# Output projections of a decoder trunk: where their sums, rests, norm and loads stand in the queues

## The chip, the cores and the metric

One core of a Trainium2 chip runs the whole program. The metric is the device time of one execution in microseconds; the median of several runs is compared. TensorE (PE) multiplies, VectorE (DVE), ScalarE (ACT) and GpSimd (POOL) do the elementwise work, and SyncE (SP) starts most transfers. Each engine works through its own queue in order.

## The reference

x is 1024 rows of 1024 float32. There are two layers; the first has sparse attention, the second dilated attention over shared keys and values. What the change touches is the end of the attention and what follows it:

```python
    o = ...                                   # attention, (B, S, D_MODEL)
    mix = o.reshape(B, S, D_MODEL).astype(h.dtype) @ w_out
...
        x = x + mix.astype(x.dtype)
        x = x + swiglu(rmsnorm(x, norm_ffn[layer]), ffn_w_up[layer], ffn_w_down[layer]).astype(x.dtype)
    return rmsnorm(x, final_norm)

def rmsnorm(x, g):
    x32 = x.astype(jnp.float32)
    y = x32 * lax.rsqrt(jnp.mean(x32 * x32, axis=-1, keepdims=True) + RMS_EPS)
    return (y * g.astype(jnp.float32)).astype(x.dtype)
```

## The kernel before

**The projection as seven products.** Each layer's output projection (`out_proj`, from L1232) multiplies the attention's output, 1024 by 1024, with w_out in seven products of half the size instead of eight. `out_steps` (L1184) lists them: B11, B21, T1, T2, B22, T3, T4. The steps T1 to T3 and B22 need sums of the quarters of the attention's output; these are made by VectorE (L1226 to L1229), each in the `sums` argument of its step. Sums of the weights are made long before and lie in DRAM (`wS`).

**A block.** Each step has four blocks i, one for each 128 columns of its left operand. A block is four banks of PSUM, one for each 128 rows, with three matmuls a bank, so twelve matmuls of 128x512 (`mm3`, L203 to L205). Three, since both operands are split (`Pairs`, L900): ScalarE writes a rounded copy, "ph" (L910), and then another engine writes what the rounding left, "pl", called the **rest** here (L911). L203 multiplies copy with copy and needs no rest; L204 and L205 need them. The rests of the left operands, and of the weights of B11, B21 and B22, are VectorE's; those of the weights of T1 to T4 are POOL's (`made(t, nc.gpsimd)`), 16 a layer.

**The order of the work.** `staged` (L917) calls the preparation of a step and then the matmuls of the step before. Within an engine the program is not run in the order written: the framework simulates it with its own costs and puts each instruction into its engine's queue where that simulation has it, so a sum that needs only the attention's output may stand in VectorE's queue far ahead of the blocks that it is for. `after(x)` (L192) makes what is issued under it stand behind x in that order. Steps of one `group` share the banks dx0 to dx3 (group 0: B11, T2, T3, T4) or dr0, dr1, ux, uy (group 1: B21, T1, B22). After a step's last block VectorE adds each bank to the residual xr (L1217), and that add frees the bank for the next step. Step T4 (`whole=True`) is run bank by bank.

**The loads.** `load` fetches four weights of a step into a ring of 16 buffers "ow"; `rows` fetches tiles of xr. Both go through SP's queue, in the order B11, four tiles of xr, B21, T1, the other four tiles, T2, B22, T3, T4, unless the simulation moves them.

**The norm and the feed-forward.** `Blocks.half` (L1006) normalises four tiles of 128 rows: for each tile one square with its row sum on ScalarE (L1023), one on VectorE (L1024), an add (L1026), a square root on ScalarE (L1027), a reciprocal (L1028), and a scaling of each half (L1029 VectorE, L1030 ScalarE). Then TensorE transposes the tiles (L1002), and copies and rests (L165, L166) make the operands B11 and B21 of the feed-forward. `half` is called six times: in both output projections for the first four tiles (prepared between T3 and T4), in both feed-forwards for the other four (`ffn`, L1265), and twice at the end of layer 0 for the projections of layer 1 (`begin_B`, `project_B`). The feed-forward's first product is L1098; L1282 scales its weights by the norm's gain on POOL while the output projection runs. `dense` (L1409) opens eight banks by name and calls `out_proj`, then `ffn`. In layer 1 the attention's last part, with merges on VectorE and POOL (L1749, L1750), overlaps the first blocks of the projection.

Of the kernel before, what the change touches and what calls it, by code (L numbers as in the profile page):

```python
# [115 lines left out]
def trunk(ctx, tc, I, out):  # L116
# [785 lines left out]
    class Pairs:  # L902
# [5 lines left out]
        def __call__(self, src, eng=None):  # L908
            h, l = [self.p.tile([128, 512], F32R, name=n_, bufs=self.n) for n_ in ("ph", "pl")]
            nc.scalar.activation(h, src, AF.Copy)  # L910
            (eng or nc.vector).tensor_sub(l, src, f32(h))  # L911
            return h, l
# [74 lines left out]
    class Blocks:  # L987
# [18 lines left out]
        def half(self, xr, hf, banks, xn, junk=None, sums=None):  # L1006
# [4 lines left out]
            junk = junk or xn  # L1011

            def prep():
# [5 lines left out]
                for j in range(4):  # L1019
                    xt = xr[:, 4 * hf + j, :]  # L1020
                    ss = cst.tile([128, 2], F32, name="nss2", bufs=8)
                    rs = ss[:, 0:1]
                    nc.scalar.activation(junk[0][j], xt[:, lo], AF.Square, accum_out=rs)  # L1023
                    nc.vector.tensor_tensor_reduce(out=junk[1][j], in0=xt[:, hi], in1=xt[:, hi], scale=1.0, scalar=0.0,  # L1024
                                                   op0=OP.mult, op1=OP.add, accum_out=ss[:, 1:2])
                    nc.vector.tensor_add(rs, rs, ss[:, 1:2])  # L1026
                    nc.scalar.activation(rs, rs, AF.Sqrt, bias=eps, scale=1.0 / D)  # L1027
                    nc.vector.reciprocal(rs, rs)  # L1028
                    nc.vector.tensor_scalar(xn[0][j], xt[:, lo], rs, None, op0=OP.mult)  # L1029
                    nc.scalar.activation(xn[1][j], xt[:, hi], AF.Copy, scale=rs)  # L1030
                    if hf == 0:
                        self.rs.append(rs)
# [8 lines left out]
            return prep  # L1041
# [142 lines left out]
    def out_steps(spare, pairs, tmp, blocks, right, xr):  # L1184


        held = {}
        n = len(blocks)
        S_ = [tmp(i) for i in range(n)]

        def step(left, name, group, first, where, sums=None, whole=False):
            def operands(i):
                if sums is not None:
                    sums(i, *blocks[i])
                return pairs(left(i)), right(name, i)

            def prep():
                ready = [operands(0)]

                def run():  # L1200
# [8 lines left out]
                    for i, t in order:  # L1209
# [4 lines left out]
                        if i == n - 1:  # L1214
                            r, c = where
                            xs = xr[:, 4 * r + t, c * 512:(c + 1) * 512]
                            nc.vector.tensor_add(xs, xs, banks[t])  # L1217
# [14 lines left out]
    def out_proj(layer, pw, pp, p, xr, oT, w, x_src, norm):  # L1232
        pairs, made = Pairs(pp, 6), Pairs(p, 4)
        raw = {}

        def load(name):
            r, c = dict(B11=(0, 0), B21=(1, 0), B22=(1, 1), T1=(0, 0), T3=(0, 1), T4=(1, 0), T2=(1, 1))[name]
            cols = slice(c * 512, (c + 1) * 512)
            for i in range(4):
# [610 lines left out]
```

## Time and profile before

| what | value |
|---|---|
| median of 3 runs | 2850.45 us (2848.82 to 2853.51) |
| the profiled execution | 2848.69 us, of which the span is 2846.9 us |
| mean granted clock of TensorE | 0.987 |
| busy: PE, DVE | 2762.8 us (97%), 2234.1 us (78%) |
| busy: ACT, POOL | 1439.8 us (51%), 1467.4 us (52%) |
| layer 0: projection's first matmul, T4's first, feed-forward's first | 680.49, 757.76, 775.07 us |
| layer 1: the same | 2073.03, 2164.39, 2181.50 us |

Times in the views count from the start of the span. A row of the timeline has its start, its duration, engine, line and operation, and in brackets the idle time of the engine before it with what ended it. The granted clock is a share of the full clock. Where a row groups several instructions, their count stands behind an x.

### The profile page before, as it was taken

Reading aid. Unit: us, or ns where it says so; the run is one execution under the profiler, and the core shown is the slowest. Engines: PE = TensorE matmul, PEld = TensorE weight load, DVE = VectorE, ACT = ScalarE, POOL = GpSimd, SP = SyncE. Lnnn points to the kernel's source line nnn. Section 1 sums busy time; section 2 is a strip of 40 time slices with the busy share of each in tenths; the row PEclk is TensorE's granted clock in tenths of the full one; section 3 lists DMA queues with packets and bytes.
Section 4 is the critical chain, followed back from the end, with each engine's and each line's share of the span. In section 5 each row is a group of like instructions: output and inputs, shape, how many; then the busy total and the mean of one; then the engine's idle time right before and its main releaser. Section 6 shows DMA issues by size and latency. Waiting matters only on the chain.

```text
span 2846.9 us, 43111 instructions
## 1 busy us (share of the span) xinstructions
PE 2762.8 (97%) x14494; PEld 2234.4 (78%) x14494; DVE 2234.1 (78%) x4563; ACT 1439.8 (51%) x3174; POOL 1467.4 (52%) x1502
## 2 busy tenths in 40 slices
PE   9999999998999999999999999999989999999997
PEld 8988676776778888888778888777767788888886
DVE  5443888886878899989875877588888889888986
ACT  5431777774554343334464444577746434343434
POOL 3135655552665566556556787100035655655652
PEclk9999999999999999999999999999999999999998
DMA  8669443214022322231223555886440211111112
GB/s 245 203 205 294 113 127 104 73 49 168 25 71 67 85 64 67 62 81 58 77 81 106 172 158 156 261 240 183 125 150 26 71 60 54 54 56 60 52 45 78
DMA packets 292926, 315.15 MB, mean 111 GB/s; under 512 B 50428, under 2 KB 229677, under 8 KB 292704
## 3 DMA queue, kind: packets, MB, share of 16 engines
q1 hardware_dynamic: 272240, 249.40, 29.2%
q0 software_dynamic: 20464, 62.99, 7.2%
q8 instruction: 115, 1.88, 0.3%
q14 instruction: 107, 0.88, 0.1%
HBM read 243.96 MB, written 81.95 MB: 114 GB/s over the span
## 4 chain that ended last, share of the span: by engine, by line
PE 84%; DVE 7%; ACT 2%; issue 2%; POOL 1%; DMA 1%; SPq 1%; DVEq 0%; ACTq 0%; POOLq 0%
PE ux L1098 18%; PE uy L1098 14%; PE dx L950 7%; PE o L364 7%; PE pt L327 6%; PE dr L950 5%; PE dr L1098 4%; PE mm L203 3%; PE mm L204 3%; PE mm L205 3%; DVE pl L911 2%; PE s L746 2%; PE dx L1098 1%; PE s L834 1%; PE s L1678 1%
## 5 line engine op out<-in xcount | busy, mean ns | idle before, releaser
L911 DVE TENSOR_TENSOR pl<-oT,ph 128x512 fp32r<-128x512 f32 x337 | 352.2, 1062 | 73.9 <-PE dr L950 17.2
L910 ACT ACTIVATE ph<-oT 128x512 fp32r<-128x512 f32 x347 | 211.9, 627 | 206.7 <-PE ux L1098 53.4
L911 DVE TENSOR_TENSOR pl<-oTb,ph 128x512 fp32r<-128x512 f32 x233 | 213.0, 937 | 28.3 <-PE dr L950 17.3
L327 PE MATMUL pt<-ident,P 128*128 128x128 f32 x1536 | 229.5, 279 | 5.4 <-POOL P L730 2.5
L910 ACT ACTIVATE ph<-oTb 128x512 fp32r<-128x512 f32 x239 | 145.5, 627 | 169.5 <-PE ux L1098 53.0
L327 PEld LDWEIGHTS pt<-ident,P 128*128 128x128 f32 x1536 | 174.0, 141 | 64.8 <-issue 42.6
L730 POOL TENSOR_SCALAR P<-P,sm,gates 128x384 f32<-128x384 f32 (+7 forms) x256 | 183.1, 727 | 77.1 <-DVE sm L728 57.3
L955 DVE TENSOR_TENSOR xr<-xr,dr 128x512 f32<-128x512 f32 x320 | 204.0, 679 | 17.8 <-PE dr L950 17.6
L955 DVE TENSOR_TENSOR xr<-xr,dx 128x512 f32<-128x512 f32 x320 | 204.6, 678 | 2.6 <-PE dx L950 2.6
L1282 POOL TENSOR_TENSOR oT<-oT,gffn 128x512 f32<-128x512 f32 x92 | 112.7, 1234 | 146.6 <-DMA oT<-in_ffn_w_up_dram 104.7
L726 ACT ACTIVATE P<-P,m 128x384 f32<-128x384 f32 (+7 forms) x256 | 170.6, 668 | 34.4 <-DVE m L839 14.0
L330 DVE COPY pT<-pt 128x512 f32<-128x512 f32 (+1 forms) x224 | 143.3, 649 | 48.6 <-PE pt L327 45.9
L330 ACT COPY pT<-pt 128x512 f32<-128x512 f32 x192 | 110.0, 577 | 112.1 <-PE pt L327 111.7
L1282 POOL TENSOR_TENSOR oTb<-oTb,gffn 128x512 f32<-128x512 f32 x92 | 110.2, 1206 | 106.3 <-DMA oTb<-in_ffn_w_up_dram 81.5
L364 PE MATMUL o<-pT,V 128*64 128x256 f32 x1200 | 160.6, 391 | 2.4 <-ACT pT L330 1.8
L1660 ACT ACTIVATE P<-P,st 128x384 f32<-128x384 f32 (+2 forms) x256 | 139.4, 546 | 30.7 <-DVE st L1655 28.8
L1655 DVE CUSTOM_DVE_ANT_0 P<-s,T 128x384 f32<-128x384 f32 (+2 forms) x256 | 112.3, 478 | 9.8 <-PE pt L327 4.4
L364 PEld LDWEIGHTS o<-pT,V 128*64 128x64 f32 x1200 | 73.8, 136 | 52.2 <-issue 10.0
L950 PE MATMUL dx<-ph 128*128 128x512 f32 x320 | 107.5, 390 | 0.4 <-ACT ph L910 0.4
L835 DVE CUSTOM_DVE_ANT_0 P<-s,T 128x128 f32<-128x128 f32 (+3 forms) x192 | 99.7, 550 | 10.3 <-PE s L834 10.1
L950 PE MATMUL dx<-ph,pl 128*128 128x512 f32 x320 | 107.0, 389 | 0.0
L910 ACT ACTIVATE ph<-wd 128x512 fp32r<-128x512 f32 x86 | 53.6, 627 | 100.6 <-PE ux L1098 48.6
(620 smaller groups left out, 8227.0 us busy)
## 6 DMA issues: line engine op xcount, KB each, us to landing
qB<-xr POOLq DMA_DIRECT2D x96, 256.0 KB, 4.9
oT<-in_ffn_w_up_dram SPq DMA_DIRECT2D x92, 256.0 KB, 2.9
oTb<-in_ffn_w_up_dram SPq DMA_DIRECT2D x92, 256.0 KB, 2.9
Q<-qB SPq DMA_DIRECT2D x40, 512.0 KB, 5.9
wd<-in_ffn_w_down_dram SPq DMA_DIRECT2D x66, 256.0 KB, 2.6
oT<-in_b_w_q_dram SPq DMA_DIRECT2D x48, 256.0 KB, 4.0
K<-kBs SPq DMA_DIRECT2D x40, 256.0 KB, 8.4
wraw<-in_a_w_in_dram SPq DMA_DIRECT2D x18, 512.0 KB, 7.0
```

Source lines behind the costliest of these rows:

```text
L327: prev = nc.tensor.transpose(ps[:, i * 128:(i + 1) * 128], h, ident)
L330: copy(t[:, :w], ps[:, :w])
L364: mm = nc.tensor.matmul(po[64 * e:64 * e + 64, :256], v[e], t, start=first and lo == i == 0, stop=last and hi == nb and i == len(ops) - 1, ...
L726: nc.scalar.activation(P[:, e, :n], P[:, e, :n], AF.Exp, bias=mm[:, e:e + 1], scale=-1.0, accum_out=sm[:, e:e + 1])
L730: nc.gpsimd.tensor_scalar(P[:, e, :n], P[:, e, :n], sm[:, e:e + 1], gate(e), op0=OP.mult, op1=OP.mult)
L910: nc.scalar.activation(h, src, AF.Copy)
L911: (eng or nc.vector).tensor_sub(l, src, f32(h))
L950: nc.tensor.matmul(banks[t], part(a, t)[u], b[v], start=z == 0 and onX != 2, stop=z == 2, skip_group_check=True)
L955: nc.vector.tensor_add(xs, xs, banks[t])
L1098: mm = nc.tensor.matmul(b, x[:, i * 128:(i + 1) * 128], ys[i], start=first and (z, i) == (0, 0), stop=(z, i) == (2, 3), skip_group_check=True)
L1282: nc.gpsimd.tensor_mul(v, v, gains[:, k:k + 4].unsqueeze(2).to_broadcast([128, 4, 128]))
L1660: nc.scalar.activation(P[:, e, :n], P[:, e, :n], AF.Exp, bias=stats[:, slot, hh:hh + 1], scale=-1.0, accum_out=stats[:, slot, 4 + hh:5 + hh])
```

## The change

1. **Sums queue behind rests.** In `out_steps` the sums and the operands of a block of step k are issued behind the rest of the same block of step k - 1.
2. **Rests of weight sums** are made by VectorE, not POOL; their ring has five buffers, not four.
3. **The norm in two parts** in the output projection: the squares are issued as one stage, the statistics and scalings as the next, behind the last add of T3 (`added[0]`). The feed-forward's first steps are issued behind that add too.
4. **One statistic for four tiles** in all six calls: eight squares on ScalarE write one tile of 128x8, then there is one add, one square root and one reciprocal for four tiles.
5. **Another place for loads and sums**: the weights B11, B21 and the first of T1 are loaded ahead of xr; the sums' tiles lie in another pool.
6. The bank dx3 is the fourth that is opened, not the seventh.

```diff
             nc.scalar.activation(h, src, AF.Copy)
-            (eng or nc.vector).tensor_sub(l, src, f32(h))
+            self.last = (eng or nc.vector).tensor_sub(l, src, f32(h))
             return h, l
...
-        def half(self, xr, hf, banks, xn, junk=None, sums=None):
+        def half(self, xr, hf, banks, xn, junk=None, sums=None, added=None):
...
+            def squares():
+                ss = cst.tile([128, 8], F32, name="nss2", bufs=2)
+                for j in range(4):
+                    for h in range(2):
+                        nc.scalar.activation(junk[h][j], xr[:, 4 * hf + j, h * 512:(h + 1) * 512], AF.Square,
+                                             accum_out=ss[:, 4 * h + j:4 * h + j + 1])
+                return ss
+            def scaled(ss):
+                rs = ss[:, 0:4]
+                nc.vector.tensor_add(rs, rs, ss[:, 4:8])
+                nc.scalar.activation(rs, rs, AF.Sqrt, bias=eps, scale=1.0 / D)
+                nc.vector.reciprocal(rs, rs)
...
+            def ahead():
+                self.ss = squares()
+                return lambda: None
...
+                with after(added and added[0]):
+                    scaled(self.ss if added else squares())
...
-            return prep
+            return prep if added is None else (ahead, prep)
...
             def operands(i):
-                if sums is not None:
-                    sums(i, *blocks[i])
-                return pairs(left(i)), right(name, i)
+                k = names.index(name)
+                with after(done.get((k - 1, i))):
+                    if sums is not None:
+                        sums(i, *blocks[i])
+                    a = pairs(left(i))
+                    done[k, i] = pairs.last
+                    return a, right(name, i)
...
-                            nc.vector.tensor_add(xs, xs, banks[t])
+                            add = nc.vector.tensor_add(xs, xs, banks[t])
+                            if name == "T3":
+                                added[0] = add
...
-        pairs, made = Pairs(pp, 6), Pairs(p, 4)
+        sums = [pw.tile([128, 512], F32, name=f"ta{i}") for i in range(4)]
+        pairs, made = Pairs(pp, 6), Pairs(p, 5)
...
-            return pairs(t) if name[0] == "B" else made(t, nc.gpsimd)
+            return pairs(t) if name[0] == "B" else made(t)
...
         load("B11")
+        load("B21")
+        load("T1", range(1))
         rows(range(4))
-        load("B21")
-        load("T1")
+        load("T1", range(1, 4))
         rows(range(4, NT))
...
-        staged(steps[:6] + [norm] + steps[6:])
+        staged(steps[:6] + list(norm) + steps[6:])
...
+                us[0] = [(n, lambda f=f: behind(f)) for n, f in us[0]]
...
-            c.push(open_banks(*[(n,) for n in ("dx0", "dx1", "dx2", "dr0", "dr1", "ux", "dx3", "uy")]))
+            c.push(open_banks(*[(n,) for n in ("dx0", "dx1", "dx2", "dx3", "dr0", "dr1", "ux", "uy")]))
```

**How the queues change.** VectorE's queue at the start of layer 0's projection, before; L848 is the attention's last copy, oT its output, ow a weight, ta the sums of T1, and L1229 makes sums of T3:

```order
L848 COPY oT<-o 128x2x128
L1226 TENSOR_TENSOR ta_8894<-oT 128x512
L1226 TENSOR_TENSOR ta_8895<-oT 128x512
L1226 TENSOR_TENSOR ta_8896<-oT 128x512
L1226 TENSOR_TENSOR ta_8897<-oT 128x512
L911 TENSOR_TENSOR pl<-oT,ph 128x512
L1229 TENSOR_TENSOR oT<-oT 128x512 x3
L911 TENSOR_TENSOR pl<-ow,ph 128x512
L1229 TENSOR_TENSOR oT<-oT 128x512
```

and now:

```order
L848 COPY oT<-o 128x2x128
L911 TENSOR_TENSOR pl<-oT,ph 128x512
L911 TENSOR_TENSOR pl<-ow,ph 128x512
L911 TENSOR_TENSOR pl<-oT,ph 128x512
L1246 TENSOR_TENSOR ta_8830<-oT 128x512
L911 TENSOR_TENSOR pl<-ow,ph 128x512
L911 TENSOR_TENSOR pl<-oT,ph 128x512
L911 TENSOR_TENSOR pl<-ow,ph 128x512
```

The first weight's rest stands second behind the copy, where seven sums and a rest stood ahead of it; the sums are strewn among later rests.

VectorE's queue at the end of T3 in layer 0, before; xn_8826 to 8829 are the norm's squares, nss its statistics, and the four adds of dx_8914 to 8917 are T3's:

```order
L1026 TENSOR_TENSOR nss_9359<-nss_9359 128x1
L911 TENSOR_TENSOR pl<-oT,ph 128x512
L1026 TENSOR_TENSOR nss_9367<-nss_9367 128x1
L1028 RECIPROCAL nss_9351<-nss_9351 128x1
L1026 TENSOR_TENSOR nss_9375<-nss_9375 128x1
L1217 TENSOR_TENSOR xr<-xr,dx_8914 128x512
L1028 RECIPROCAL nss_9359<-nss_9359 128x1
L1029 TENSOR_SCALAR xn_8822<-xr,nss_9351 128x512
L1028 RECIPROCAL nss_9367<-nss_9367 128x1
L1217 TENSOR_TENSOR xr<-xr,dx_8915 128x512
L1029 TENSOR_SCALAR xn_8823<-xr,nss_9359 128x512
L1217 TENSOR_TENSOR xr<-xr,dx_8916 128x512
```

and now:

```order
L1235 TENSOR_TENSOR xr<-xr,dx_8914 128x512
L911 TENSOR_TENSOR pl<-ow,ph 128x512
L1235 TENSOR_TENSOR xr<-xr,dx_8915 128x512
L1235 TENSOR_TENSOR xr<-xr,dx_8916 128x512
L1235 TENSOR_TENSOR xr<-xr,dx_8917 128x512
L1024 TENSOR_TENSOR nss_9351<-nss_9351 128x4
L1235 TENSOR_TENSOR xr<-xr,dx_8914 128x512
L1026 RECIPROCAL nss_9351<-nss_9351 128x4
L1029 TENSOR_SCALAR xn_8822<-xr,nss_9351 128x512
```

T3's adds stand ahead of the norm's statistics; the second add of dx_8914 is T4's.

SP's queue at layer 1's projection, before; the wS rows are weights of T3 and T4, xS holds the residual:

```order
L1241 DMA ow<-in_b_w_out_dram 128x512 x8
L1241 DMA ow<-wS_82 128x512 x8
L1241 DMA ow<-in_b_w_out_dram 128x512 x4
L1241 DMA ow<-wS_82 128x512
L1250 DMA xr<-xS 128x1024 x8
L1241 DMA ow<-wS_82 128x512 x4
```

and now:

```order
L1262 DMA ow<-in_b_w_out_dram 128x512 x8
L1262 DMA ow<-wS_82 128x512 x8
L1262 DMA ow<-in_b_w_out_dram 128x512 x4
L1262 DMA ow<-wS_82 128x512 x4
L1271 DMA xr<-xS 128x1024 x8
L1262 DMA ow<-wS_82 128x512 x4
```

The loads of xr stand behind three more loads of weights.

More of the change, by code (lines that the diff above doesn't have):

```diff
@@ L1018, in prep @@
                     self.rs = []
[L1019 to L1032, printed above, removed]
+                with after(added and added[0]):
+                    scaled(self.ss if added else squares())
                 def run():
@@ L1230, in out_steps, with out_proj, load @@
                 step(A(3), "T4", 0, False, (1, 0), whole=True)]
-    def out_proj(layer, pw, pp, p, xr, oT, w, x_src, norm):
-        pairs, made = Pairs(pp, 6), Pairs(p, 4)
+    def out_proj(layer, pw, pp, p, xr, oT, w, x_src, norm, added):
+        sums = [pw.tile([128, 512], F32, name=f"ta{i}") for i in range(4)]
+        pairs, made = Pairs(pp, 6), Pairs(p, 5)
         raw = {}
-        def load(name):
+        def load(name, parts=range(4)):
             r, c = dict(B11=(0, 0), B21=(1, 0), B22=(1, 1), T1=(0, 0), T3=(0, 1), T4=(1, 0), T2=(1, 1))[name]
             cols = slice(c * 512, (c + 1) * 512)
-            for i in range(4):
+            for i in parts:
                 t = raw[name, i] = pw.tile([128, 512], F32, name="ow", bufs=16)
@@ L1260, in out_proj, with ffn @@
         blocks = [(oT[:, i, lo], oT[:, i, hi], oT[:, i + 4, lo], oT[:, i + 4, hi]) for i in range(4)]
-        steps = out_steps(("dr0", "dr1", "ux", "uy"), pairs, lambda i: p.tile([128, 512], F32, name=f"ta{i}"), blocks,
-                          right, xr)
-        staged(steps[:6] + [norm] + steps[6:])
-    def ffn(p, scratch, B, xr, layer):
+        steps = out_steps(("dr0", "dr1", "ux", "uy"), pairs, lambda i: sums[i], blocks,
+                          right, xr, added)
+        staged(steps[:6] + list(norm) + steps[6:])
+    def ffn(p, scratch, B, xr, layer, added):
         up, down = I["ffn_w_up"][layer], I["ffn_w_down"][layer]
@@ L1367, in ffn, with behind @@
                 early = [us[1], pairs_of[2][1][0]]
+                def behind(f):
+                    with after(added[0]):
+                        return f()
+                us[0] = [(n, lambda f=f: behind(f)) for n, f in us[0]]
                 us[0] = [("", f) for f in B.first_steps(us[0], norm, [f for c in early for _, f in c[:2]])]
@@ L1420, in dense @@
                 pw, pp, p = [pool(c2, n, near) for n in ("fow", "fop", "fo")]
-                out_proj(layer, pw, pp, p, xr, oT, w, x_src, B.half(xr, 0, ("dr0", "dr1", "ux", "uy"), places(p)))
+                added = [None]
+                norm = B.half(xr, 0, ("dr0", "dr1", "ux", "uy"), places(p), added=added)
+                out_proj(layer, pw, pp, p, xr, oT, w, x_src, norm, added)
             with ExitStack() as cu:
```

13 lines of the change are left out of this document (10 added, 3 removed).

## The prediction

> **What bounds the kernel now.** I read the page first, then the list of TensorE's waits, then windows and the timeline around the largest of them.
>
> ```profile
> span 2846.9 us, 43111 instructions
> PE 84%; DVE 7%; ACT 2%; issue 2%; POOL 1%; DMA 1%; SPq 1%; DVEq 0%; ACTq 0%; POOLq 0%
> ```
>
> TensorE carries 84% of the chain; the change takes no matmul away, so it can win only time in which TensorE stands still or runs at a low granted clock. The waits name the places (line and operand, releaser, total us, times, longest):
>
> ```profile
> PE dx L204 <- DVE pl L911: 9.6, 2, 4.8
> PE dx L203 <- DVE nss L1028: 7.9, 2, 4.0
> ...
> PE dx L203 <- DVE o L1749: 1.3, 1, 1.3
> ```
>
> All three lie in the two output projections: L204 at their start, "nss L1028" at the start of step T4. Each also costs clock. The windows (us, busy us of each engine with counts, then the granted clock), layer 0 first:
>
> ```profile
> core 0: us, PE busy (x) PEld busy (x) DVE busy (x) ACT busy (x) POOL busy (x), PEclk, DMA share, GB/s
> 680.00:690.00 10.00, 5.18 (x18) 3.61 (x15) 8.85 (x15) 2.33 (x6) 0.00 (x0) 0.76 0.97 363
> 690.00:700.00 10.00, 10.00 (x41) 8.13 (x40) 5.40 (x10) 4.66 (x9) 1.35 (x1) 0.90 1.04 413
> ...
> 750.00:760.00 10.00, 6.03 (x22) 4.66 (x21) 10.00 (x18) 4.77 (x10) 6.80 (x5) 0.85 0.09 27
> 760.00:770.00 10.00, 10.00 (x46) 8.23 (x45) 7.39 (x11) 6.34 (x13) 9.42 (x8) 0.81 0.00 0
> ```
>
> and layer 1:
>
> ```profile
> 2080.00:2090.00 10.00, 8.25 (x43) 4.17 (x41) 7.47 (x13) 3.86 (x8) 2.74 (x3) 1.00 0.01 2
> 2090.00:2100.00 10.00, 5.53 (x16) 4.06 (x16) 10.00 (x9) 3.45 (x6) 9.52 (x6) 0.83 0.48 165
> 2100.00:2110.00 10.00, 8.68 (x31) 7.01 (x32) 10.00 (x18) 2.31 (x4) 0.00 (x0) 0.83 1.03 410
> ...
> 2160.00:2170.00 10.00, 6.03 (x17) 4.55 (x16) 10.00 (x17) 6.68 (x13) 8.33 (x7) 0.66 0.10 27
> ```
>
> What the clock took is busy time by the missing share: layer 0, 5.18 x 0.24 + 10 x 0.10 = 2.2 us at the start and 6.03 x 0.15 + 10 x 0.19 = 2.8 us at T4; layer 1, 5.53 x 0.17 + 8.68 x 0.17 = 2.4 us and 6.03 x 0.34 = 2.1 us: 9.5 us in all.
>
> **The start of layer 0.** The timeline (start, duration, what; in brackets the idle time before):
>
> ```profile
> 680.95 2.49 DVE L1226 TENSOR_TENSOR ta<-oT 128x512 f32<-128x512 f32 x4
> 683.95 1.89 DVE L1229 TENSOR_TENSOR oT<-oT 128x512 f32<-128x512 f32 x3
> 685.76 0.68 DVE L911 TENSOR_TENSOR pl<-ow,ph 128x512 fp32r<-128x512 f32 x1
> 686.50 0.80 PE L204 MATMUL dx<-pl,ph 128*128 128x512 f32 x1 [4.82 <-DVE pl L911]
> 687.09 0.63 PE L205 MATMUL dx<-ph,pl 128*128 128x512 f32 x1
> 687.51 0.63 PE L204 MATMUL dx<-pl,ph 128*128 128x512 f32 x1
> ```
>
> Four sums of T1 and three of T3, of no use until later, pass VectorE before the first weight's rest, and TensorE waits 4.82 us; afterwards matmuls start 0.42 us apart. One VectorE operation takes (2.49 - 0.68) / 3 = 0.60 us from start to start. The new order has the attention's copy and one rest ahead of that rest, so it ends at 680.95 + 2 x 0.60 = 682.2; four matmuls that need no rest cover part of it, and I keep 0.8 us of the wait. The weights of B21 now leave SP ahead of four x rows and of three of T1's weights, which arrive later but are read later too.
>
> **The start of T4.**
>
> ```profile
> 752.27 0.39 PE L203 MATMUL dx<-ph 128*128 128x512 f32 x1
> ...
> 753.40 0.39 PE L205 MATMUL dx<-ph,pl 128*128 128x512 f32 x1
> 757.76 0.77 PE L203 MATMUL dx<-ph 128*128 128x512 f32 x1 [3.97 <-DVE nss L1028]
> ```
>
> ```profile
> 756.94 0.68 DVE L1217 TENSOR_TENSOR xr<-xr,dx 128x512 f32<-128x512 f32 x1
> ```
>
> The first two rows are five starts apart: 0.226 us a matmul. The releaser named is the reciprocal, but what T4 needs is its bank, emptied by the add of 756.94, which stood in VectorE's queue behind the norm's squares, sums and reciprocals. Now T3's four adds stand ahead of the norm. A T3 block takes 12 x 0.226 = 2.7 us and VectorE needs 0.60 us for the add of a bank, so the stall of 3.97 us goes. Next late are the copies and rests of B11, which follow sixteen transposes that now stand near T4's end: a copy and a rest, about 0.6 us each as above, beside three last matmuls: I keep 1.5 us.
>
> **Layer 1** has the same two places, and the end of attention between:
>
> ```profile
> 2090.99 0.50 PE L203 MATMUL dx<-ph 128*128 128x512 f32 x1 [1.29 <-DVE o L1749]
> ...
> 2101.32 0.50 PE L204 MATMUL dx<-pl,ph 128*128 128x512 f32 x1 [4.80 <-DVE pl L911]
> ```
>
> ```profile
> 2090.86 4.17 DVE L1226 TENSOR_TENSOR ta<-oTb 128x512 f32<-128x512 f32 x3
> 2094.95 3.45 DVE L1229 TENSOR_TENSOR oTb<-oTb 128x512 f32<-128x512 f32 x2
> 2098.32 1.75 DVE L911 TENSOR_TENSOR pl<-oTb,ph 128x512 fp32r<-128x512 f32 x1
> ```
>
> Here a sum takes 1.39 us, since POOL works beside it (9.52 us of 10 in the window). In the new order the rests of B11's blocks 2 and 3 and of B21's first two stand among the merge's operations, and two whole blocks of matmuls move into the attention's end; they fill the idle 1.75 us of 2080 to 2090 and the 1.29 us. What is late next: a rest of a B21 weight six rows behind the last merge add (6 x 0.60 = 3.6 us, against 18 matmuls, 4.1 us, plus one POOL operation beside it): 1.0 us. Then x:
>
> ```profile
> 2094.92 4.21 SPq L1250 DMA_DIRECT2D xr<-xS  x8
> ```
>
> ```profile
> xr<-xS SPq DMA_DIRECT2D x8, 512.0 KB, 7.3
> ```
>
> These eight loads now stand behind all four of T3's weights instead of one, so behind eight freed slots; the last is freed by a rest two rows behind the last merge add, near 2096 in the new timing. Landing takes 7.3 us at the median, so the first rows land at 2100 to 2104; VectorE's first add of x stands ten rows behind the merge, near 2102, with the rests of T2's left sides queued behind it. Price 0 to 4 us; I take 1.5. The adds of B21's banks sit eight rows further, 8 x 0.60 = 4.8 us, while TensorE has about nine matmuls to do meanwhile: 1.5 us more. And 1.5 us at B11, as in layer 0.
>
> **VectorE's load.** Sixteen rests a layer come to it from POOL. Groups of 693 to 753 us (count, then busy and mean ns):
>
> ```profile
> L911 POOL TENSOR_TENSOR pl<-ow,ph 128x512 fp32r<-128x512 f32 x13 | 20.6, 1606 | 17.8 <-ACT ph L910 17.8
> ...
> L911 DVE TENSOR_TENSOR pl<-oT,ph 128x512 fp32r<-128x512 f32 x15 | 12.9, 873 | 6.5 <-ACT ph L910 6.5
> ...
> L1282 POOL TENSOR_TENSOR oT<-oT,gffn 128x512 f32<-128x512 f32 x7 | 8.5, 1219 | 11.3 <-DVE xr L1217 6.3 <-DMA oT<-in_ffn_w_up_dram 5.0
> ...
> L911 DVE TENSOR_TENSOR pl<-ow,ph 128x512 fp32r<-128x512 f32 x8 | 7.8, 974 | 4.7 <-PE dx L204 2.5 <-ACT ph L910 2.1
> L911 DVE TENSOR_TENSOR pl<-ta,ph 128x512 fp32r<-128x512 f32 x8 | 6.3, 802 | 3.5 <-ACT ph L910 1.8 <-PE uy L204 1.6
> ...
> L1217 DVE TENSOR_TENSOR xr<-xr,dx 128x512 f32<-128x512 f32 x8 | 5.0, 681 | 0.0
> ```
>
> From T1 to T3's last add the new order has 69 VectorE operations in layer 0, 69 x 0.60 = 41.4 us, against 16 blocks of 2.7 us on TensorE, 43.4 us. What POOL costs beside it: over an undisturbed 0.68 us the rests lost 15 x 0.19 + 8 x 0.29 + 8 x 0.12 = 6.2 us to 29.1 us of POOL work, 0.21 us for one. POOL keeps the seven of L1282, 8.5 us: 1.8 us. 41.4 + 1.8 = 43.2 us: it fits, with nothing left over. I take no cost.
>
> **The norm elsewhere** is called four times outside. All eight squares now run on ScalarE, and one statistic serves four tiles, so the transposes wait for the last tile. The place to watch is the end of layer 0's feed-forward:
>
> ```profile
> 1431.59 0.44 PE L1002 MATMUL dx<-ident,oT 128*128 128x128 f32 x2 [1.22 <-DVE oT L1048]
> ```
>
> ```profile
> 1431.91 1.06 ACT L165 ACTIVATE B11h<-dr 128x512 fp32r<-128x512 f32 x2
> ```
>
> By the new ScalarE order four squares of the second half (0.6 us and a read each) stand ahead of those copies and two Sqrt fewer: the copies come about 2 us later, with TensorE idle until then; one microsecond of transposes leaves that place. Bound -2 (VectorE is freed of eight squares) to +3; I take +1. The other calls: 0, between -3 and +3.
>
> **Sum**, against the profiled execution's 2848.7 us: waits 4.82 + 3.97 + 4.80 + 1.29 + 3.97 = 18.9; idle filled 1.75; clock 9.5; together 30.1 us. Kept: 0.8 + 1.5 in layer 0, 1.0 + 1.5 + 1.5 + 1.5 in layer 1, 7.8 us, without clock, since each is short and stands amid dense matmuls. Elsewhere +1. Net 21.3 us: 2827.4 us. The median of the runs shown is 1.8 us above the profiled one, so 2827 to 2829; I say 2827.5.
>
> The Trainium skill, "TensorE: Matmul & The Clock Gate", Part 1, has the clock at half until about 3.4 us of activity have passed. By that the restarts at five waits would cost 1.7 us each, 8.5 us, an estimate, and the time would be 1 us longer; the windows decide, with 2.1 to 2.8 us for a restart.
>
> **Rivals.**
> 1. POOL holds VectorE up (0.13). If each of the seven L1282 stops it for its whole length, VectorE needs 41.4 + 8.5 = 49.9 us for 43.4: 6.5 us a layer, 13 us, and 2840 us. For it: the sums at 1.39 us beside a full POOL. Against: 0.21 us lost for one of POOL, since adds from PSUM (681 ns) lose nothing. The Trainium skill, "SBUF — State Buffer", Who interferes with whom, says exactly this: an operation of VectorE with two SBUF inputs and a GpSimd operation that reads SBUF shut each other out entirely. The trace agrees for single operations, not for the stretch.
> 2. x comes late in layer 1 (0.11): the full 4 us wait instead of 1.5 and a restart of 2.4 us: 2832.5 us; with the slots freed later still, 2836.
> 3. VectorE becomes the bound and the clock falls (0.11): slower than before. If its operations take a mean of 0.78 us instead of 0.60, the 69 need 53.8 us, 10.4 over a layer, and the 21 us are gone; at 0.87 us, what rests from oT took on average, 60.0 us, 16.6 a layer: 2827.4 + 33 = 2860, more if each block's wait lowers the clock. For it: that mean. Against: two thirds of POOL's work there leaves.
> 4. More than forecast (0.10): no wait is kept and the other calls gain 3: 2816.
>
> My forecast has 0.55. The range reaches over 1, 2 and 4: 2814 to 2843. About 0.2% (5.7 us) is what a measurement here can tell from none. Faster 0.89; same 0.05 and slower 0.06 split rival 3 by its point.
>
> **What would show it.** The waits "L204 <- pl L911" and "L203 <- nss L1028" gone or under 1.5 us; granted clock 1.00 at both T4 starts; the first feed-forward product of layer 0 some 13 us sooner after the projection's first matmul. A string of short waits for L911 from T1 to T3 is rival 1 or 3; a VectorE wait for a DMA on xr in layer 1 is rival 2. If those waits go and the time does not follow, my reading of what bounds the stretch is wrong.

## The result, and the profile after

The changed kernel takes 2828.86 us (median of 4 runs, 2825.47 to 2831.03), the kernel before 2850.30 us on the same chip. The ratio on record is 0.9922, with a 95% interval of 0.9905 to 0.9939; the two medians alone divide to 0.9925. The prediction was 2827.5. One run of e10, an experiment below, took 4141.87 us at a mean granted clock of 0.61, and no ratio counts it. The profiled execution took 2828.26 us, with a span of 2826.5 us, 20.4 less than before. In the changed kernel's lines L1217 is L1235, L1250 is L1271, L1282 is L1304, L1098 is L1111, L1048 is L1061, L1749 is L1778; L203 to L911 and L1002 stay.

The chain by engines, from the page:

```profile
span 2826.5 us, 43085 instructions
PE 85%; DVE 6%; ACT 4%; issue 1%; DMA 1%; SPq 1%; POOL 1%; DVEq 0%; ACTq 0%; POOLq 0%
```

TensorE's waits (total us, times, longest):

```profile
PE ux L1111 <- DVE B21l L166: 2.2, 2, 1.3
...
PE dx L1111 <- ACT B11h L165: 1.0, 2, 0.8
...
PE dx L204 <- DVE pl L911: 0.6, 1, 0.6
```

Of the 9.6 us of L204 waiting for a rest 0.6 is left; L203 waiting for the norm's statistics is gone. The feed-forward's first operands (B11h, B21l) are what is late now. The windows, in the columns of the prediction:

```profile
680.00:690.00 10.00, 9.40 (x41) 7.46 (x41) 8.05 (x14) 5.32 (x10) 0.00 (x0) 1.00 1.02 401
690.00:700.00 10.00, 10.00 (x46) 8.28 (x45) 9.78 (x17) 3.74 (x8) 0.00 (x0) 1.00 1.00 387
750.00:760.00 10.00, 9.84 (x51) 7.87 (x49) 7.03 (x9) 8.42 (x18) 7.38 (x6) 1.00 0.00 1
...
2090.00:2100.00 10.00, 9.18 (x39) 7.09 (x39) 10.00 (x16) 3.46 (x6) 2.97 (x2) 1.00 0.56 197
...
2160.00:2170.00 10.00, 9.09 (x55) 7.53 (x54) 10.00 (x15) 9.49 (x19) 5.98 (x5) 1.00 0.01 2
700.00:750.00 50.00, 49.95 (x221) 41.06 (x220) 46.25 (x70) 31.44 (x67) 20.41 (x12) 1.00 0.22 64
```

The granted clock is 1.00 where it was 0.66 to 0.90. From 700 to 750 us, B21 to T3, TensorE stands still for 0.05 us, and VectorE, with the rests that were POOL's, has 3.75 us of 50 to spare. The timeline at the places of the prediction:

```profile
759.36 0.99 PE L1111 MATMUL dx<-B11h,ph 128*128 128x512 f32 x2 [0.16 <-ACT B11h L165]
...
770.58 1.20 PE L1111 MATMUL ux<-B21h,ph 128*128 128x512 f32 x4 [1.30 <-DVE B21l L166]
...
785.46 1.19 PE L1111 MATMUL uy<-T1h,ph 128*128 128x512 f32 x4 [1.01 <-DVE oT L1132]
```

T4 starts without a wait and needs no row; B11 waits 0.16 us. The two last rows lie in the feed-forward's start, whose idle time grows (below).

To set the forecast's terms against the measurement I use the feed-forward's first product as a mark, and its step T4 as a second. Before, each layer in turn up to the first mark, then from the first to the second:

```profile
2073.00:2181.50 108.50, 96.30 (x426) 75.29 (x425) 87.58 (x144) 49.95 (x103) 52.78 (x37) 0.94 0.23 80
...
680.50:775.10 94.60, 85.81 (x371) 70.29 (x369) 76.10 (x121) 47.25 (x93) 46.74 (x33) 0.93 0.36 132
775.10:811.60 36.50, 33.39 (x175) 26.75 (x173) 28.52 (x42) 26.00 (x49) 20.64 (x17) 1.00 0.20 58
2181.50:2217.60 36.10, 33.43 (x175) 26.74 (x173) 27.28 (x41) 26.11 (x49) 20.68 (x17) 1.00 0.20 59
```

and the same stretches after:

```profile
2067.50:2159.15 91.65, 88.12 (x410) 69.33 (x408) 78.85 (x131) 50.99 (x109) 29.89 (x21) 1.00 0.27 95
...
679.80:759.40 79.60, 78.79 (x355) 64.57 (x353) 70.60 (x107) 48.52 (x100) 27.79 (x17) 1.00 0.40 141
759.40:800.10 40.70, 35.87 (x188) 28.41 (x188) 32.76 (x44) 28.13 (x52) 21.15 (x17) 1.00 0.18 52
2159.15:2198.30 39.15, 35.53 (x188) 28.26 (x188) 30.60 (x42) 27.47 (x50) 20.38 (x16) 1.00 0.19 55
```

The second number is the length, the third TensorE's busy time; their difference is its idle time. One thing moved over the mark: sixteen transposes of the norm's second half stood ahead of the first product, and now stand among its matmuls. Before, the last four of them ahead of the mark at 775.07; then after, the first four behind the mark at 759.36:

```profile
774.72 0.60 PE L1002 MATMUL uy<-ident,xn 128*128 128x128 f32 x4
```

```profile
760.18 0.60 PE L1002 MATMUL dr<-ident,xn 128*128 128x128 f32 x4
```

One transpose alone takes 0.27 us and four take 0.60, so they start 0.11 us apart, and sixteen are 1.75 us. In the table this is taken out: it is no gain ahead of the mark and no loss behind it.

| stretch, us | forecast | measured |
|---|---|---|
| layer 0, idle time | 2.3 - 8.8 = -6.5 | 0.8 - 8.8 = -8.0 |
| layer 0, clock | -5.0 | 78.8 - 85.8 + 1.75 = -5.3 |
| layer 0, start of the feed-forward | 0 | 40.7 - 36.5 - 1.75 = +2.4 |
| layer 1, idle time | 5.5 - 11.8 = -6.3 | 3.5 - 12.2 = -8.7 |
| layer 1, clock | -4.5 | 88.1 - 96.3 + 1.75 = -6.4 |
| layer 1, start of the feed-forward | 0 | 39.15 - 36.1 - 1.75 = +1.3 |
| all the rest | +1 | +4.3, what is left to -20.4 |
| sum | -21.3 | -20.4 |

### The profile page after: what moved, and what is told of

The parts are those of the page before. It is cut to its first block, busy times and chain, and to the rows that moved or that the text cites. A ratio compares the mean times of both kernels' runs of the same rounds, so it can differ in the third digit from the quotient of the medians.

```text
span 2826.5 us, 43085 instructions
## 1 busy us (share of the span) xinstructions
PE 2748.7 (97%) x14494; PEld 2222.0 (79%) x14494; DVE 2222.9 (79%) x4511; ACT 1448.0 (51%) x3204; POOL 1419.9 (50%) x1470
## 3 DMA queue, kind: packets, MB, share of 16 engines
q8 instruction: 115, 1.88, 0.3%
## 4 chain that ended last, share of the span: by engine, by line
PE 85%; DVE 6%; ACT 4%; issue 1%; DMA 1%; SPq 1%; POOL 1%; DVEq 0%; ACTq 0%; POOLq 0%
PE ux L1111 18%; PE uy L1111 15%; PE dx L950 8%; PE o L364 7%; PE pt L327 6%; PE dr L950 5%; PE dr L1111 4%; PE mm L204 2%; PE mm L203 2%; PE mm L205 2%; DVE pl L911 2%; PE s L746 1%; PE s L834 1%; PE dx L1111 1%; PE s L833 1%
## 5 line engine op out<-in xcount | busy, mean ns | idle before, releaser
L911 DVE TENSOR_TENSOR pl<-oT,ph 128x512 fp32r<-128x512 f32 x337 | 352.4, 1062 | 75.8 <-PE dr L950 17.4
L911 DVE TENSOR_TENSOR pl<-oTb,ph 128x512 fp32r<-128x512 f32 x233 | 212.6, 935 | 28.0 <-PE dr L950 17.4
L1304 POOL TENSOR_TENSOR oT<-oT,gffn 128x512 f32<-128x512 f32 x92 | 117.3, 1286 | 192.7 <-DMA oT<-in_ffn_w_up_dram 136.6
L1304 POOL TENSOR_TENSOR oTb<-oTb,gffn 128x512 f32<-128x512 f32 x92 | 110.4, 1209 | 128.7 <-DMA oTb<-in_ffn_w_up_dram 83.3
```

Source lines behind the costliest of these rows:

```text
L911: self.last = (eng or nc.vector).tensor_sub(l, src, f32(h))
L1304: nc.gpsimd.tensor_mul(v, v, gains[:, k:k + 4].unsqueeze(2).to_broadcast([128, 4, 128]))
```

## The experiments

The table holds every run: the ratio of times to the kernel before on the same chip, then from the run's profile the span, and TensorE's time in three stretches. "Layer 0" and "layer 1" run from the projection's first matmul to the feed-forward's T4, "between" from one to the other.

| run | ratio (95%) | span | layer 0 | between | layer 1 |
|---|---|---|---|---|---|
| before | 1 | 2846.9 | 131.1 | 1261.5 | 144.6 |
| before, again | one run, 2846.17 us | 2844.4 | 130.9 | 1264.4 | 143.3 |
| changed kernel | 0.9922 (0.9905 to 0.9939) | 2826.5 | 120.3 | 1267.4 | 130.8 |
| changed, again | 0.9922 (0.9909 to 0.9936) | 2822.9 | 120.1 | 1265.6 | 130.8 |
| e1, sums free | 0.9958 (0.9943 to 0.9973) | 2837.0 | 127.1 | 1270.0 | 133.1 |
| e5, loads as before | 0.9965 (0.9953 to 0.9977) | 2840.1 | 127.4 | 1270.1 | 134.9 |
| e9, both | 0.9964 (0.9950 to 0.9977) | 2838.5 | 127.6 | 1270.5 | 133.1 |
| e3, norm in one stage | 0.9923 (0.9908 to 0.9938) | 2825.3 | 120.8 | 1268.3 | 130.4 |
| e7, a statistic for each tile | 0.9962 (0.9951 to 0.9973) | 2831.5 | 125.1 | 1264.3 | 134.6 |
| e8, one statistic alone | 1.0003 (0.9994 to 1.0013) | 2849.2 | 130.1 | 1268.0 | 143.6 |
| e2, rests on POOL | 0.9952 (0.9934 to 0.9970) | 2827.5 | 119.4 | 1263.6 | 137.0 |
| e10, banks as before | 0.9935 (0.9912 to 0.9959) | 2829.3 | 119.8 | 1270.2 | 134.1 |
| e4, old norm elsewhere | 0.9936 (0.9918 to 0.9954) | 2830.8 | 121.7 | 1265.1 | 135.0 |
| e6, old norm at layer 0's end | 0.9922 (0.9909 to 0.9934) | 2821.3 | 121.0 | 1262.9 | 131.1 |

**Scatter.** The unchanged files were run again.

> The changed kernel itself, once more, to stand beside the others on the same chip and to show what differs between two of its profiles. Ratio to before 0.992 as before (0.9905 to 0.9939). Open from the first profile: the stretch from the query projections' T2 product (1447 us) to layer 1's first projection matmul took 620.4 us against 616.7 before, with the same order of matmuls. If that is chance, this profile shows another length, by 2 us or more; if it belongs to the change, it is again 620 to 622 us.

> The kernel before, once more, for a second profile of it. Open: from the query projections' T2 product to layer 1's first projection matmul it took 616.7 us, and 620.4, 621.0 and 618 to 622.7 us in the changed kernel and its variants, with the same order of matmuls. If 616.7 is chance, the second profile shows 619 us or more; if it belongs to the kernel before, 616 to 618 us, and the change costs some 4 us there.

The two layers repeat to 0.2 us in the changed kernel and to 0.2 and 1.3 us in the one before; "between" differs by 1.9 and 2.9 us for the same code. So, as far as two profiles of each kernel can tell, a difference of 2 us in a layer means something, and one of 2 us in between doesn't. The result itself repeats. The stretch that was asked about, from the query projections' T2 product to layer 1's projection, took 621.0 us in the changed kernel and 618.7 us in the kernel before: the first is what was expected of a cost of the change, the second lies between the two answers.

**The start of layer 0.** My theory was that the order of the sums is the whole of it. e1 sets the sums free again.

```diff
-                with after(done.get((k - 1, i))):
+                with after(None):
```

> The changed kernel without the order between sums and rests; all else stays. In VectorE's queue of layer 0 four sums of T1 and three of T3 stand ahead of the first weight's rest again. My theory (the starts of the projections waited for sums): the waits of L204 for the rest come back, 4.0 us or more in each layer (4.82 and 4.80 before, 0.60 now in layer 0), with a slow clock behind each (2.2 and 2.4 us in the windows of before), so 2829 + 8 + 4 = about 2841 us, 2837 to 2844. Rival (the starts waited for the loads of the weights, which the change also moved): the new loads alone keep the gain, and the time stays within 3 us of 2829.

```profile
683.18 0.80 PE L204 MATMUL dx<-pl,ph 128*128 128x512 f32 x1 [3.89 <-DVE pl L911]
```

The wait is back in layer 0, which is longer by 6.8 us. In layer 1, against the expectation, no such wait comes back, and the layer is longer by 2.3 us. e5 keeps the new order of sums and puts back the order of loads, whose effect the prediction gave no price.

```diff
         load("B11")
-        load("B21")
-        load("T1", range(1))
         rows(range(4))
-        load("T1", range(1, 4))
+        load("B21")
+        load("T1")
```

> The changed kernel with the loads in the order of before: four tiles of xr ahead of the weights of B21. My theory (sums were the wait, loads are second): in layer 0 the copies of B21's weights come at 687.5 instead of about 684, when B11's blocks are nearly done; 0 to 3 us of wait in layer 0, nothing in layer 1, where the weights are there long before: 2829 to 2833 us, 2830 as one number. Rival (the loads were half of the wait): 4 us or more and a slow clock in layer 0: 2835 us or more.

Layer 0 is longer by 7.1 us though L204 waits only 0.60 us as in the changed kernel. (Layer 1, where nothing was expected, is longer by 4.1 us: TensorE waits 1.01 us at T4 and 1.41 us at B11, and the feed-forward's start takes 1.4 us more.) TensorE, then ScalarE, then SP's queue in e5, and SP's queue in the changed kernel:

```profile
687.29 0.97 PE L203 MATMUL dr<-ph 128*128 128x512 f32 x2 [4.09 <-ACT ph L910]
```

```profile
686.61 0.63 ACT L910 ACTIVATE ph<-ow 128x512 fp32r<-128x512 f32 x1 [7.23 <-DMA ow<-in_a_w_out_dram]
```

```profile
677.26 1.75 SPq L1271 DMA_DIRECT2D xr<-in_x_dram  x4
679.05 2.47 SPq L1262 DMA_DIRECT2D ow<-in_a_w_out_dram  x4
```

```profile
608.90 58.29 SPq L1262 DMA_DIRECT2D ow<-in_a_w_out_dram  x8
```

In e5 the loads of x leave at 677.26. B21's weights stand behind them, leave at 679.05 and are there at 686.6; in the changed kernel they are issued with B11's, from 608.90 on. In the kernel before they left at 680.19, and ScalarE's copy of the first of them waited for its load while TensorE stood in its 4.82 us:

```profile
687.53 0.63 ACT L910 ACTIVATE ph<-ow 128x512 fp32r<-128x512 f32 x1 [6.98 <-DMA ow<-in_a_w_out_dram]
```

So two waits stood at this place, and TensorE's rows of before show only the one that ended last. e9 takes back both.

> The changed kernel with both undone: the order between sums and rests, and the order of the loads. Each alone cost some 10 us, of which 6.8 and 7.1 us lie between layer 0's first projection matmul and its feed-forward's T4 product. My theory (the two waits stand side by side at layer 0's start: while TensorE waits 4 us for a rest behind the sums, the late weights of B21 arrive): together they cost there what one does, 7 to 9 us, 127 to 129 us for that stretch; total 10 to 13 us over the changed kernel. Rival (they follow each other): 14 us there, 134 us, and 18 us or more over it in total.

```profile
685.34 0.79 PE L204 MATMUL dx<-pl,ph 128*128 128x512 f32 x1 [4.82 <-DVE pl L911]
```

e1 127.1, e5 127.4, both 127.6: each costs alone what both cost together. They lie side by side in time, as e9's theory had it, and in layer 0 either part of the change without the other is worth nothing here. The theory with which this series began, that the sums are the whole of it, fell with e5.

**The start of T4.** Here I held that the place of the norm behind T3's adds matters. e3 makes the norm in one stage, and its statistics wait for no add.

```diff
-                norm = B.half(xr, 0, ("dr0", "dr1", "ux", "uy"), places(p), added=added)
+                norm = [B.half(xr, 0, ("dr0", "dr1", "ux", "uy"), places(p))]
```

> The changed kernel with the norm of the projections as one stage between T3 and T4, not behind T3's last add; still one statistic for four tiles. In VectorE's queue one add, one reciprocal and four scalings stand ahead of T3's first add of a bank. My theory (T4 waits for that add behind the norm): a wait of 1.5 to 4 us at the start of T4 in each layer, and about 2 us of slow clock behind each where it is over 3 us: 2833 to 2841 us, 2836 as one number. Rival (it was the number of statistics that cost: four square roots and adds, not the place): one statistic is enough, no wait at T4 over 1 us, and the time stays within 2 us of 2829.

Nothing is lost (120.8 and 130.4 us), and yet in layer 0 the norm's add, its reciprocal and the four scalings now stand ahead of T3's first add. VectorE, the scalings and then that add:

```profile
743.38 2.46 DVE L1029 TENSOR_SCALAR xn<-xr,nss 128x512 f32<-128x512 f32 x4
745.76 0.67 DVE L1235 TENSOR_TENSOR xr<-xr,dx 128x512 f32<-128x512 f32 x1
```

T4 starts 2.87 us behind the start of T3's last matmul, where the changed kernel has 0.43 us. But sixteen of the norm's transposes stand in that time, which TensorE has to do anyway, and it is idle there for 0.44 us only. In layer 1 the add and the reciprocal alone stand ahead of T3's first add, and T4 waits 0.25 us. e7 does the opposite: two stages and the place behind the add, but for each tile a square on VectorE, an add, a square root and a reciprocal of its own.

```diff
-                self.ss = squares()
+                self.ss = []
+                for j in range(4):
+                    xt = xr[:, 4 * hf + j, :]
+                    ss = cst.tile([128, 2], F32, name="nss1", bufs=8)
+                    nc.scalar.activation(junk[0][j], xt[:, lo], AF.Square, accum_out=ss[:, 0:1])
+                    nc.vector.tensor_tensor_reduce(out=junk[1][j], in0=xt[:, hi], in1=xt[:, hi], scale=1.0, scalar=0.0,
+                                                   op0=OP.mult, op1=OP.add, accum_out=ss[:, 1:2])
+                    self.ss.append(ss)
```

> The changed kernel, but in the output projections a statistic for each tile and half of the squares on VectorE, in two parts and behind T3's last add as now. One statistic in one part alone already kept the whole gain at T4. Theory: either of the two is enough, since T3's adds stand ahead of the four adds and reciprocals here too: no wait over 1 us at T4, the scaled tiles come 1 to 2 us later, and T4's end covers that; the ratio of the changed kernel within 0.001. Rival (the statistic is what matters: four square roots one behind the other with adds and reciprocals delay the transposes): a wait of 1 to 3 us ahead of the transposes in each layer, 2 to 6 us over the changed kernel.

First T4's wait in layer 0 for T3's add (L1253) in e7, then the last of the four VectorE squares (L1040) ahead of that add:

```profile
746.74 0.47 PE L203 MATMUL dx<-ph 128*128 128x512 f32 x1 [2.11 <-DVE xr L1253]
```

```profile
743.00 1.78 DVE L1040 CUSTOM_DVE_ANT_0 xn<-xr 128x512 f32<-128x512 f32 x1
```

The squares stay ahead of the adds, and both layers lose (4.8 and 3.8 us). In layer 0 T4's wait is under half of that; B11, which waits 0.16 us in the changed kernel, waits longer still:

```profile
762.05 2.07 PE L1129 MATMUL dx<-B11h,ph 128*128 128x512 f32 x4 [2.39 <-ACT B11h L165]
```

So the place of the statistics behind T3's add is neither needed (e3) nor enough (e7). What keeps the gain at both is one statistic for four tiles with all squares on ScalarE; which of these two does it was not parted. e8 gives the kernel before this one part alone.

```diff
+                ss = cst.tile([128, 8], F32, name="nss2", bufs=2)
+                for j in range(4):
+                    for h in range(2):
+                        nc.scalar.activation(junk[h][j], xr[:, 4 * hf + j, h * 512:(h + 1) * 512], AF.Square,
+                                             accum_out=ss[:, 4 * h + j:4 * h + j + 1])
+                rs = ss[:, 0:4]
+                nc.vector.tensor_add(rs, rs, ss[:, 4:8])
+                nc.scalar.activation(rs, rs, AF.Sqrt, bias=eps, scale=1.0 / D)
+                nc.vector.reciprocal(rs, rs)
```

> The kernel before with one part of the change alone: one statistic for four tiles and all squares on ScalarE, in all six norms, in one part as before. Theory: T4's waits go (3.97 us twice, with 2.8 and 2.1 us of slow clock), and some of that is lost again behind it, in the feed-forward's start, where the second norm's work comes into the open: 3.5 us gained in layer 0 between the first projection matmul and the T4 product (131.1 us before, so 127 to 128 us), about 6 us in layer 1; the waits of L204 stay at 4 to 5 us each: ratio 0.9955 to 0.998. Rival (the T4 waits need the order behind T3's add): the waits stay at 2 us or more and the ratio is 0.998 to 1.001.

```profile
PE dx L204 <- DVE pl L911: 11.2, 2, 6.4
```

```profile
789.49 0.77 PE L1002 MATMUL dr<-ident,oT 128*128 128x128 f32 x5 [1.20 <-POOL oT L1061]
...
792.15 0.44 PE L1002 MATMUL dr<-ident,oT 128*128 128x128 f32 x2 [1.24 <-POOL oT L1061]
```

T4's wait is gone from the list, and yet the time is that of before. As in e3, sixteen transposes stand between T3 and T4, here with 1.28 us of idle time. In layer 0 the feed-forward starts 4.8 us earlier (89.8 us behind the projection's first matmul, not 94.6) but its T4 only 1.0: two waits of 1.2 us for POOL stand between, where the kernel before has one of 0.89, and the granted clock from one to the other is 0.96 instead of 1.00. In layer 1 the wait of L204, the longer of the two in the row above, is 6.4 us and not 4.80. That is no effect of e8: the second profile of the kernel before has 6.38 us there too.

**Rests and layer 1.** e2 gives the sixteen rests back to POOL.

```diff
-            return pairs(t) if name[0] == "B" else made(t)
+            return pairs(t) if name[0] == "B" else made(t, nc.gpsimd)
```

> The changed kernel, but the 16 rests a layer of the weights' sums are POOL's again. My theory (VectorE had room for them, and POOL's own work beside VectorE cost more than it relieved): VectorE's operations beside POOL become longer again, TensorE waits little for it in layer 0 (0 to 2 us), more in layer 1, where POOL's rests fell on the merge: 1 to 4 us there; 2 to 6 us over the changed kernel, a ratio of 0.993 to 0.9945. Rival (VectorE is nearly full from T1 to T3, as I reckoned 43.2 of 43.4 us, and each operation less helps): 1 to 3 us faster than the changed kernel.

Layer 0 loses nothing (119.4 us), layer 1 6.2 us, more than the 1 to 4 us that I expected. The largest wait there, what VectorE does ahead of it, and POOL:

```profile
2134.25 0.50 PE L204 MATMUL dr<-pl,ph 128*128 128x512 f32 x1 [2.02 <-DVE pl L911]
```

```profile
2125.28 1.17 DVE L911 TENSOR_TENSOR pl<-oTb,ph 128x512 fp32r<-128x512 f32 x1
2126.37 1.78 DVE L1249 TENSOR_TENSOR oTb<-oTb 128x512 f32<-128x512 f32 x1
...
2134.11 1.88 DVE L911 TENSOR_TENSOR pl<-oTb,ph 128x512 fp32r<-128x512 f32 x3
```

```profile
2124.86 1.04 POOL L1304 TENSOR_TENSOR oTb<-oTb,gffn 128x512 f32<-128x512 f32 x1 [4.86 <-DVE xr L1235]
2125.86 1.75 POOL L911 TENSOR_TENSOR pl<-ow,ph 128x512 fp32r<-128x512 f32 x1
...
2130.71 2.93 POOL L1304 TENSOR_TENSOR oTb<-oTb,gffn 128x512 f32<-128x512 f32 x2
```

Beside POOL an operation of VectorE takes 1.2 to 1.8 us; once POOL has stopped at 2133.6, three take 1.88. So it is layer 1 alone that gains by the move of the rests, and at this wait it gains by POOL's absence. The next largest wait there, 1.91 us at B11 (0.81 in the changed kernel), was not followed back. e10 opens the banks in the order of before.

```diff
-            c.push(open_banks(*[(n,) for n in ("dx0", "dx1", "dx2", "dx3", "dr0", "dr1", "ux", "uy")]))
+            c.push(open_banks(*[(n,) for n in ("dx0", "dx1", "dx2", "dr0", "dr1", "ux", "dx3", "uy")]))
```

> The changed kernel with the banks opened in the order of before (dx3 seventh). In TensorE's queue of layer 1, 30 fewer matmuls of the projection then stand ahead of the last merge matmul of the attention. My theory: those 30 x 0.226 = 6.8 us filled the attention's last waits, so without them 3 us of idle and about 2 us of slow clock come back in layer 1: 133 to 136 us from layer 1's first projection matmul to its feed-forward's T4 product against 130.8 us, nothing in layer 0, 3 to 6 us over the changed kernel. Rival (the rests earlier in VectorE's queue fill that place, the bank does not matter): 0 to 1 us.

Layer 0 as in the changed kernel (119.8 us), layer 1 longer by 3.3 us, with a wait in the attention's end that the changed kernel doesn't have:

```profile
2085.37 0.50 PE L203 MATMUL dx<-ph 128*128 128x512 f32 x1 [1.29 <-DVE o L1778]
```

It is the 1.29 us that the kernel before had there. But the changed kernel has waits of 1.00 and 0.70 us in its place (their rows stand in the next section): over the first 28 us of the projection TensorE is idle for 2.99 us in e10 and 2.24 in the changed kernel. So 0.75 of the 3.3 us show there; 1.5 us lie in the feed-forward's start, and why is not shown. The interval of the ratio doesn't part this kernel from the changed one.

**The norm elsewhere.** e4 takes back the old norm (per tile, squares on both engines) in the four other calls, e6 in the two at the end of layer 0 that prepare layer 1's projections.

```diff
-                    scaled(self.ss if added else squares())
...
+                else:
+                    for j in range(4):
...
+                        nc.scalar.activation(junk[0][j], xt[:, lo], AF.Square, accum_out=rs)
+                        nc.vector.tensor_tensor_reduce(out=junk[1][j], in0=xt[:, hi], in1=xt[:, hi], scale=1.0, scalar=0.0,
```

> The changed kernel, but the four norms outside the output projections (two in the feed-forwards, two at the end of layer 0) have a statistic for each tile, with half of the squares on VectorE, as before the change. My theory: the gain in the projections was 28 us and not 21; one statistic for four tiles took some 5 us back outside, 2.5 us between the first feed-forward product of layer 0 and 816 us, and 2.3 us between 1383 and 1447 us: 2822 to 2826 us, 2824 as one number. Rival (those losses come from the earlier start itself, work that used to be hidden behind the stalls): they stay, and the time is 2829 us within 2 us.

> The changed kernel, but the two norms at the end of layer 0 have a statistic for each tile with half of the squares on VectorE, as before the change; the feed-forwards keep one statistic. My theory, from the stretches of the run with all four old norms (from the feed-forward's T4 product to the query projections' T2 product 644.2 us against 647.0 now; the feed-forwards 1 and 4 us slower): 2.8 us less there and nothing lost elsewhere, so a ratio 0.001 under that of the changed kernel on this chip, about 0.991. Rival (the 2.8 us are lost again in the attention's waits for its loads, as leads before it were): the same ratio as the changed kernel within 0.0005.

e4 gains nothing: layer 0 is 1.4 us longer, layer 1 4.2. In both layers transposes behind T4 now wait 1.7 us for one of the differences that VectorE makes for the feed-forward's step T1, and B11 waits 1.20 and 0.95 us. I had expected part of the rest's +4 back; it came out of "between" (1265.1 against 1267.4 and 1265.6) no further than chance reaches. e6 has the shortest span and "between" of all changed kernels, but its time over five runs is the changed kernel's. No experiment made a version that is faster than the changed kernel.

## Why the prediction was right, and which steps were not

The total held (21.3 us forecast, 20.4 and, in the repeated pair, 2844.4 - 2822.9 = 21.5 measured), and so did the mechanism: the waits in the two projections, and the clock that they cost. But steps were wrong by up to 4 us a stretch, and that they cancelled in the total is luck.

**The start of layer 0.** Kept: 0.60 us of the wait, forecast 0.8. The clock: -5.3 against -5.0 for both places. But the step "which arrive later but are read later too", which left the loads without a price, missed that loads were half of the cause: for B21's weights a second wait stood hidden behind the first. Had the change not moved them, the forecast's gain in layer 0 would have been 7 us too large.

**T4.** The stall went, as forecast, and the clock is 1.00. The reason given was that the adds stand ahead of the norm. That order is neither needed nor enough: in e3 the norm stands ahead of the adds again and nothing is lost, and in e7 the statistics stand behind the adds and a wait of 2.11 us comes back, with the squares on VectorE. What the prediction passed over at this place is the other part of the change, one statistic with the squares on ScalarE; it priced that part for the calls elsewhere alone. Of the 1.5 us kept at B11, 0.16 stayed in layer 0 and 0.81 in layer 1:

```profile
2159.15 1.22 PE L1111 MATMUL dx<-B11h,ph 128*128 128x512 f32 x4 [0.81 <-ACT B11h L165]
```

**The start of the feed-forward** had a 0 in the sum, and costs 2.4 and 1.3 us. The B11 copies were priced as the next late thing; what is late are the ones behind them, B21's rest (1.30 us) and the sums of T1 (1.01 us). My reading is that TensorE reaches them earlier than VectorE can, and that T4's stall hid this work before the change. e8 agrees: without the stall its feed-forward takes 40.3 us from its first product to T4, against 36.5. It isn't the whole of it, since in e4, with the old norm there, the waits lie ahead of the first product instead.

**Layer 1** gained 15.1 us up to the feed-forward's first product, and 13.7 in the repeated pair, where I forecast 10.8. Rival 2, with its 1.5 us in the forecast, didn't come. SP's queue, then VectorE's first add of x:

```profile
2094.32 4.24 SPq L1271 DMA_DIRECT2D xr<-xS  x8
```

```profile
2098.62 0.68 DVE L1235 TENSOR_TENSOR xr<-xr,dx 128x512 f32<-128x512 f32 x1
```

The slots were free at 2094.3, not 2096, and the add follows the queue's order without a wait 4.3 us after the first issue, where I took 7.3 for landing. The rest of a B21 weight, which I gave 1.0 us, makes no wait. The banks that I gave 1.5 us cost 0.25:

```profile
2103.55 0.50 PE L203 MATMUL dr<-ph 128*128 128x512 f32 x1 [0.25 <-DVE xr L1235]
```

Of the attention's end I had forecast all 3.04 us of idle time filled. I counted 0.3 us of that twice, since the wait that ends at 2090.99 begins ahead of 2090. And waits of 1.00 and 0.70 us stayed:

```profile
2087.07 0.50 PE L203 MATMUL uy<-ph 128*128 128x512 f32 x1 [1.00 <-DVE oTb L1697]
...
2090.93 0.50 PE L203 MATMUL dr<-ph 128*128 128x512 f32 x1 [0.70 <-DVE oTb L1778]
```

And the clock cost 6.4 us, not 4.5. I had taken the right three slices, but multiplied the mean of each by its busy time, as if the slow clock lay evenly over busy and idle time. The clock of before is reduced in three stretches, and there it is at one half:

```profile
2091.54:2094.95 3.41, 3.41 (x9) 2.63 (x8) 3.41 (x4) 2.30 (x4) 3.41 (x3) 0.50 0.20 76
2101.78:2105.19 3.41, 3.41 (x10) 2.63 (x9) 3.41 (x7) 0.84 (x2) 0.00 (x0) 0.50 1.02 416
2163.22:2170.05 6.83, 5.66 (x15) 4.55 (x16) 6.83 (x13) 5.61 (x11) 5.16 (x5) 0.50 0.03 7
```

TensorE is busy for 12.48 of these 13.65 us, and half of that is 6.2 us. The share varies: in the repeated pair the clock cost 4.2 us in layer 1 and the idle time fell by 9.6 instead of 8.7, since the wait of L204 was 6.38 us in that profile of before.

Open: which part removed layer 1's wait of 4.80 us. It stays away with the sums free (e1), the loads as before (e5), both (e9), the rests on POOL (e2) and the banks as before (e10), each by itself. Either several parts suffice alone or it takes two of those to bring it back; pairs other than e9 were not tried.

**VectorE's load** had no price, rightly: TensorE is busy 49.95 of 50 us there in layer 0. Rivals 1 and 3 would have shown as a string of waits for L911; there is none. The argument against rival 1 was weaker than it looked, though (last section).

**Elsewhere** I took +1 with bounds of -2 to +3 at one place. By what is left over it is +4.3 in one pair of profiles and +1.8 in the other. Since "between" differs by 1.9 and 2.9 us between runs of the same code, and taking the norm back gives no measurable time, its cause stays open. Most of it lies between the query projections' T2 product and layer 1's projection: 616.7 and 618.7 us before, 620.4 and 621.0 in the changed kernel.

## What to carry to other kernels

A trace shows at each place the wait that ended last; before a wait is taken out of a sum, ask of every operand of the next instructions when it was there, and from which queue, since another wait may lie beside it and only parts that remove both gain anything. Work that is hidden by a stall has to be priced when the stall goes: here 1.3 to 2.4 us of each layer's gain came back as the next operands were late. And a total that agrees is no proof of its terms: take marks in the program, and compare idle and busy time between them.

## What the hardware showed that I had not expected

VectorE and POOL hold each other up far more than the 0.21 us for one that the prediction took from a mean. In e2, from 2125.28 to 2134.11 us, VectorE does six operations (four of them in the rows left out above) in 8.83 us, 1.47 each where 0.60 is the undisturbed start to start, while POOL does five, three of L1304 and two of L911 (two of the five left out). Alone, with VectorE idle, POOL takes 1.04 us for one of L1304 and 1.3 us for one of L911 in this run. If the two engines never ran at once, 6 x 0.60 + 3 x 1.04 + 2 x 1.3 = 9.3 us would be needed, an estimate: so in this stretch they came close to taking turns. The Trainium skill, "SBUF — State Buffer", Who interferes with whom, says that a VectorE operation with two inputs in SBUF and a GpSimd operation that reads SBUF shut each other out; here the trace agrees nearly, for a stretch of 9 us too. I take it that the changed kernel bears it because POOL keeps little work there and VectorE had time to spare.

The length of a wait does not tell what it costs in clock. In the changed kernel waits of 0.60, 0.81 and 1.30 us left the granted clock at 1.00 in the rows above. In e2 the attention's end of layer 1 has a wait of 1.29 us too, and just behind it the clock falls to one half:

```profile
2085.59 0.56 PE L203 MATMUL dr<-ph 128*128 128x512 f32 x1 [1.29 <-DVE o L1778]
```

```profile
2085.91:2089.32 3.41, 3.41 (x9) 2.65 (x8) 1.57 (x1) 0.14 (x1) 3.41 (x3) 0.50 0.23 77
```

and in e10 a wait of the same length, at 2085.37, leaves it at 1.00:

```profile
2077.20:2087.20 10.00, 7.74 (x37) 4.35 (x36) 7.56 (x13) 4.83 (x9) 5.52 (x4) 1.00 0.02 5
```

For e2 it is 3.41 x 0.50 = 1.7 us of its loss in layer 1. What parts the two was not tried, but the traces have a hint. In every one of them the clock is full or at one half, and it changes only at points that lie whole multiples of 3.41 us apart. In e2 TensorE is idle for 1.62 us of the 3.41 us that end where the clock falls, at 2085.91; in e10 such a point, at 2084.60, cuts the wait in two, and the steps on both sides of it have 1.27 and 0.77 us of idle time. So it seems to be the idle time within a step that counts. No sharp limit comes out: over all traces the clock fell behind every step with more than 1.9 us of idle time, and below that behind some and not behind others.
